# Products of the down rows of blocks 0 and 1 scheduled at high priority at their anchors

## Chip, cores and metric

The kernel runs on one core of a Trainium2 chip. The metric is the device time of one execution in microseconds (us). The kernel before takes 3732.13 us, the median of three runs (3730.72 to 3739.1).

## What is computed

One decoder layer over 1024 tokens of width 1024, all in float32. Two mixers run in parallel on the normed input (sliding-window attention with sinks, and an mLSTM in chunks), are gated, summed and projected (`w_out`), and added to the input: this is x2. Behind it stands a PEER expert layer. For every token and each of 8 heads, two lists of 128 scores give a top 16 of 16384 experts; then, cut to what matters here:

```
idx  = take_along_axis(cand_i, best_pos)                 # 8 heads x 16 experts of a token
gate = softmax(best_s)
act  = gelu(einsum('td,thkd->thk', xb, expert_down[idx]))   # the down rows
out  = einsum('thk,thkd->td', gate * act, expert_up[idx])   # the up rows
```

## The kernel before, in words

The 1024 tokens are 8 blocks of 128. The program has two parts.

**The front** goes over four groups of two blocks (0 and 1, 2 and 3, 4 and 5, 6 and 7). For each group `front` computes projections, attention, mLSTM, gates, x2 and the scores of the experts. Weights come in 512 KB parts on SP's DMA queue (L224, three buffers). In 200 of the 328 parts the weight is split: ACT rounds it (`whi`, L232), DVE takes the rest (`wlo`, L233), and TensorE (PE) runs three matmuls (L249 to L251); the others (outputs of the mixers, `w_out`, the query) go straight to L247. The last step of a group on DVE is the sum with x, L632. Behind each group's front the previous group's `topk` is written (DVE, L671 to L723) and, for blocks 2 to 5, `spread` (DVE L756 and L759 build one-hot rows, PE L764 multiplies them, the result goes to `gate_d`). `later` gives both a priority number that is 5000 larger, that is, they come after the front where both are ready.

**The dense part** (`dense`, L840 on) computes all 16384 experts for blocks 2 to 5 by matmuls (L856 and others), and beside it the gathered rows of blocks 1, 6 and 7.

Blocks 0 and 1 get their down products in the front. `down` (L777) does it: POOL gathers one expert row for each of the 128 tokens by an indirect DMA of 512 KB (L772), DVE multiplies it with xb and sums it into a column of `act` (L785), 128 times for a block. The gathers have three buffers (`gp`), so a gather waits for the product that stands three places before it. Block 1 waits for block 0 at `act` and `xb`, which have one buffer. From block 0's products come its coefficients (Gelu on ACT, L789; L790 on DVE), and `scatter` adds them into the table `coef_d` by 128 indirect DMAs from POOL (L801), in 8 heads of 16, each head after the one before has landed. Block 0 then takes part in the dense matmuls.

What sets the order: the program is written down as a trace and a list scheduler orders each engine's queue, taking among the ready instructions the one with the smallest priority number, which grows with the place in the program. The products of blocks 0 and 1 are written behind all four groups. Each carries an ordering edge (no wait on the chip) to an anchor, a matmul of the front:

```
for s in range(P):
    t = fetch(p, "down", r["idx"], s)
    ins = V.tensor_tensor_reduce(out=t, in0=t, in1=xb, ..., accum_out=act[:, s:s + 1])
    after(ins, next(pace, None))
```

The front has 664 such anchors, 166 in a group. Block 0's products are paced from 0.34 to 0.64 of them (`PACE0`, `PACE1`), block 1's from 0.64 to 0.96 (`PACE2`), the scatters from 0.66 to 0.97 (`SPREAD0`, `SPREAD1`). An anchor says only that a product does not come earlier. On the chip every engine works its queue strictly in order.

Of the kernel before, what the change touches and what calls it, by code (L numbers as in the profile page):

```python
# [23 lines left out]
P = 128  # L24
# [14 lines left out]
HALF = 0  # L39
EARLY = (1,)  # L40
# [8 lines left out]
PACE0, PACE1, PACE2 = 0.34, 0.64, 0.96  # L49
# [48 lines left out]
def build(nc, tc, a, out, dbg=None):  # L98
# [8 lines left out]
    gp = pool("gather", 3)  # L107
# [53 lines left out]
    def after(ins, name):  # L161
        if name is not None:
            tc.add_manual_dep(ins.ins, name, NOSYNC, reason="pace")
# [606 lines left out]
    def fetch(p, table, idx, s):  # L770
        t = p.tile([P, D], F32, name="g")
        G.indirect_dma_start(out=t, out_offset=None, in_=a[table],  # L772
                             in_offset=bass.IndirectOffsetOnAxis(ap=idx[:, s:s + 1], axis=0))
        return t

    def down(r, b, pace, p):
        act = bp.tile([P, P], F32, name="act", bufs=1)  # L777
        xb = bp.tile([P, D], F32, name="xb", bufs=1)
        SY.dma_start(xb, xb_d[b])
        gain = p.tile([P, D], F32, name="g")  # L780
        SY.dma_start(gain, a["gain2"].to_broadcast([P, D]))
        V.tensor_tensor(xb, xb, gain, ALU.mult)
        for s in range(P):
            t = fetch(p, "down", r["idx"], s)
            ins = V.tensor_tensor_reduce(out=t, in0=t, in1=xb, scale=1.0, scalar=0.0, op0=ALU.mult,  # L785
                                         op1=ALU.add, accum_out=act[:, s:s + 1])
            after(ins, next(pace, None))
        coef = bp.tile([P, P], F32, name="coef")
        A.activation(coef, act, AF.Gelu)  # L789
        V.tensor_tensor(coef, coef, r["gate"].rearrange("p h k -> p (h k)"), ALU.mult)  # L790
        r["coef"] = coef

    def scatter(cell, vals, pace):

        views = bass_types.dram_disjoint_views(flat[:, None], 16)
        done = []
        for h in range(8):
            new = []
            for s in range(16):
                c = 16 * h + s  # L800
                ins = G.indirect_dma_start(out=views[s], out_offset=bass.IndirectOffsetOnAxis(ap=cell[:, c:c + 1], axis=0),  # L801
                                           in_=vals[:, c:c + 1], in_offset=None, compute_op=ALU.add)
                if s == 0:
                    for d in done:
                        tc.add_manual_dep(ins.ins, d, SYNC, reason="heads")
                else:
                    after(ins, new[0])
                after(ins, next(pace, None))
                new.append(ins.ins.name)
            done = new  # L810
# [112 lines left out]
    res = {}  # L923
# [18 lines left out]
    def paced(lo, hi, n):  # L942
        return iter([names[int((lo + i * (hi - lo) / n) * len(names))] for i in range(n)])

    down(res[HALF], HALF, paced(PACE0, PACE1, P), gp)
    scatter(res[HALF]["cell"], res[HALF]["coef"], paced(SPREAD0, SPREAD1, P))
    for b in EARLY:
        down(res[b], b, paced(PACE1, PACE2, P), gp)
    inner.close()
    gd = dense()  # L950
    names = anchors["dense"]
# [19 lines left out]
```

## Time and profile before

| | |
|---|---|
| Median of three runs | 3732.13 us |
| The profiled execution | 3726.21 us, span 3724.4 us |
| Busy: PE, DVE, ACT, POOL | 87%, 74%, 36%, 37% of the span |
| Mean granted TensorE clock | 0.925 |

The profile is one execution. Busy time is by engine; idle time stands before an instruction and is put down to what ended it. `PE pj L250 <- DVE wlo L233` reads: PE waited at line 250 for what DVE writes at line 233. Times "in a stretch" are from the span's start. The stretches used below end with the last L632 of a group: group 1 is 327 to 752 us, group 2 is 752 to 1229, group 3 is 1229 to 1833; the first dense matmul starts at 1992.

### The profile page before, as it was taken

To read this page: it belongs to the slowest core of one execution; us is meant where nothing else is said; L and a number is where in the kernel's file an instruction comes from. 1 tells how busy PE (TensorE), PEld (TensorE's weight loads), DVE (VectorE), ACT (ScalarE), POOL (GpSimd) and SP (SyncE) were. 2 spreads that over 40 slices of the span, in tenths; PEclk is the share of its full clock that TensorE was granted. 3 is DMA by queue.
4 is the path that set the end of the run, shared out by engine and by line. 5 is a ranking of instruction groups with operands and counts; after the bars stand their busy time and mean duration, and the time that the engine had idled before them with its cause. 6 is when DMAs were issued, how large, how long until landed. Compare 5 with 4: busy or idle time off the path is not lost.

```text
span 3724.4 us, 49376 instructions
## 1 busy us (share of the span) xinstructions
PE 3247.9 (87%) x17248; PEld 2737.1 (73%) x17248; DVE 2762.6 (74%) x6356; ACT 1322.2 (36%) x2667; POOL 1396.2 (37%) x1028
## 2 busy tenths in 40 slices
PE   7998998779989648867567999989889999999999
PEld 7887887668778547756455777777777788777887
DVE  5331877659788347667976988878878888888886
ACT  6642664138454317321543322212212222222222
POOL 0000002310012576768000056555555555555552
PEclk9999989889899769878888999999999999999999
DMA  6444446873379867778656399989989999998995
GB/s 193 155 146 151 149 141 209 302 268 124 121 222 293 243 188 214 245 239 246 156 113 230 127 316 324 319 321 343 324 300 319 321 329 321 323 328 312 330 317 192
DMA packets 413049, 914.00 MB, mean 245 GB/s; under 512 B 179584, under 2 KB 200832, under 8 KB 408704
## 3 DMA queue, kind: packets, MB, share of 16 engines
q0 software_dynamic: 147456, 469.89, 37.4%
q1 hardware_dynamic: 265344, 440.96, 35.7%
q8 instruction: 136, 2.23, 0.2%
q14 instruction: 113, 0.93, 0.1%
HBM read 847.75 MB, written 62.98 MB: 245 GB/s over the span
## 4 chain that ended last, share of the span: by engine, by line
issue 20%; POOL 14%; DMA 12%; DVE 9%; PE 8%; ACT 1%; POOLq 0%; SPq 0%; ACTq 0%; DVEq 0%
POOL g L772 13%; DMA g<-up,idx 5%; DMA g<-down,idx 4%; PE ph L856 2%; PE at L764 1%; POOL coef_d L801 1%; DMA rawu<-up 1%; PE pj L247 1%; DVE g L785 1%; DVE ld L846 1%; PE po L886 1%; PE po L890 1%; PE po L889 1%; DVE lu L846 1%; DVE ef L711 0%
## 5 line engine op out<-in xcount | busy, mean ns | idle before, releaser
L772 POOL DMA_INDIRECT g<-down,idx x512 | 639.3, 1249 | 1469.8 <-DVE act L785 567.4
L785 DVE CUSTOM_DVE_ANT_0 g<-g,xb 128x1024 f32<-128x1024 f32 x512 | 618.7, 1222 | 347.0 <-DMA g<-down,idx 339.2
L772 POOL DMA_INDIRECT g<-up,idx x384 | 530.8, 1382 | 756.3 <-DVE y L894 371.2
L818 DVE SCALAR_TENSOR_TENSOR acc<-g,coef,acc 128x1024 f32<-128x1024 f32 x384 | 492.4, 1282 | 78.1 <-DMA g<-up,idx 68.7
L856 PE MATMUL ph<-xbh,hd 128*128 128x512 f32 x1024 | 414.0, 404 | 66.1 <-ACT hd L845 36.6
L856 PE MATMUL ph<-xbh,ld 128*128 128x512 f32 x1024 | 415.6, 406 | 33.7 <-DVE ld L846 33.6
L845 ACT CAST hu<-rawu 128x1024 fp32r<-128x1024 f32 x128 | 131.3, 1047 | 846.0 <-PE po L890 582.5
L856 PE MATMUL ph<-xbl,hd 128*128 128x512 f32 x1024 | 411.0, 401 | 0.0
L233 DVE TENSOR_TENSOR wlo<-w,whi 128x1024 fp32r<-128x1024 f32 x200 | 243.6, 1220 | 145.2 <-ACT whi L232 144.0
L232 ACT CAST whi<-w 128x1024 fp32r<-128x1024 f32 x200 | 209.2, 1047 | 392.9 <-DMA w<-wmain 246.6
L250 PE MATMUL pj<-wlo,hT 128*128 128x256 f32 x832 | 249.1, 300 | 72.7 <-DVE wlo L233 72.7
L856 PEld LDWEIGHTS ph<-xbh,hd 128*128 128x128 f32 x1024 | 200.7, 196 | 115.0 <-ACT hd L845 38.4
L856 PEld LDWEIGHTS ph<-xbh,ld 128*128 128x128 f32 x1024 | 199.8, 195 | 91.2 <-DVE ld L846 49.5
L249 PE MATMUL pj<-whi,hT 128*128 128x256 f32 x832 | 248.6, 301 | 17.5 <-ACT whi L232 17.5
L251 PE MATMUL pj<-hT,wlo 128*128 128x256 f32 x768 | 228.4, 300 | 23.9 <-DVE wlo L233 23.9
L251 PE MATMUL pj<-whi,hTlow 128*128 128x256 f32 x832 | 247.2, 298 | 0.0
L801 POOL DMA_INDIRECT coef_d<-coef,cell x128 | 225.9, 1765 | 50.6 <-issue 36.6
L249 PE MATMUL pj<-hT,whi 128*128 128x256 f32 x768 | 232.7, 304 | 8.4 <-ACT whi L232 4.3
L856 PEld LDWEIGHTS ph<-xbl,hd 128*128 128x128 f32 x1024 | 200.1, 195 | 42.4
L250 PE MATMUL pj<-hTlow,whi 128*128 128x256 f32 x768 | 228.5, 298 | 0.0
L250 PEld LDWEIGHTS pj<-wlo,hT 128*128 128x128 f32 x832 | 169.9, 204 | 76.9 <-DVE wlo L233 74.9
L846 DVE TENSOR_TENSOR lu<-rawu,hu 128x1024 fp32r<-128x1024 f32 x128 | 156.1, 1219 | 93.6 <-ACT hu L845 91.3
(290 smaller groups left out, 7666.9 us busy)
## 6 DMA issues: line engine op xcount, KB each, us to landing
w<-wmain SPq DMA_DIRECT2D x328, 512.0 KB
rawd<-downT SPq DMA_DIRECT2D x128, 512.0 KB
rawu<-up SPq DMA_DIRECT2D x128, 512.0 KB
gate_d<-stage SPq DMA_DIRECT2D x32, 1024.0 KB
g<-gate_d SPq DMA_DIRECT2D x32, 1024.0 KB
x<-x SPq DMA_DIRECT2D x16, 512.0 KB
coef_d<-none SPq DMA_DIRECT2D x128, 64.0 KB
sc_d<-sc SPq DMA_DIRECT2D x16, 512.0 KB
```

The costliest lines, as they stand in the source:

```text
L232: A.copy(hi, t)
L233: V.tensor_tensor(lo, t, hi.bitcast(F32), ALU.subtract)
L249: T.matmul(ps, lh(c), rh(c), start=first, stop=False)
L250: T.matmul(ps, lh(c), rl(c), start=False, stop=False)
L251: ins = T.matmul(ps, ll(c), rh(c), start=False, stop=last)
L772: G.indirect_dma_start(out=t, out_offset=None, in_=a[table], in_offset=bass.IndirectOffsetOnAxis(ap=idx[:, s:s + 1], axis=0))
L785: ins = V.tensor_tensor_reduce(out=t, in0=t, in1=xb, scale=1.0, scalar=0.0, op0=ALU.mult, op1=ALU.add, accum_out=act[:, s:s + 1])
L801: ins = G.indirect_dma_start(out=views[s], out_offset=bass.IndirectOffsetOnAxis(ap=cell[:, c:c + 1], axis=0), in_=vals[:, c:c + 1], in_off ...
L818: ins = V.scalar_tensor_tensor(acc, t, g, acc, ALU.mult, ALU.add)
L845: A.copy(hi, raw)
L846: V.tensor_tensor(lo, raw, hi.bitcast(F32), ALU.subtract)
L856: ins = T.matmul(ps, w[:, c, :], x[:, c, :], start=first, stop=last)
```

## The change

`down` of blocks 0 and 1 is traced in `tc.high_priority()`, so that its instructions go ahead of all others that are ready. The call of block 1 is moved in front of `scatter`. Anchors, paces, buffers and arithmetic stay.

```
-    down(res[HALF], HALF, paced(PACE0, PACE1, P), gp)
+    with tc.high_priority():
+        down(res[HALF], HALF, paced(PACE0, PACE1, P), gp)
+        for b in EARLY:
+            down(res[b], b, paced(PACE1, PACE2, P), gp)
     scatter(res[HALF]["cell"], res[HALF]["coef"], paced(SPREAD0, SPREAD1, P))
-    for b in EARLY:
-        down(res[b], b, paced(PACE1, PACE2, P), gp)
```

No instruction is added or taken away on DVE, PE, POOL or SP; the last 2069 rows of DVE's queue, 6977 of PE's and 655 of POOL's, which hold the dense part, stand as before. Counted from the two orders, DVE's queue up to the last L632 of each group holds:

| DVE rows | group 1 | group 2 | group 3 | then, up to the first dense step |
|---|---|---|---|---|
| products L785, before | 57 | 61 | 138 | 0 |
| products L785, now | 58 | 105 | 93 | 0 |
| topk + spread, before | 353 + 0 | 344 + 428 | 187 + 244 | 207 + 224 |
| topk + spread, now | 353 + 0 | 302 + 224 | 381 + 448 | 55 + 224 |

The first product stands at DVE's row 784 (before: 948), the last of block 0 at 1758 (before: 2435).

**POOL's queue from the first gather on.** The gathers are `g<-down,idx`, the scatters `coef_d<-coef,cell`. Before:

```order
L772 DMA g<-down,idx 128x1024 x128
L801 DMA coef_d<-coef,cell 2097152x1 x16
L772 DMA g<-down,idx 128x1024 x2
L801 DMA coef_d<-coef,cell 2097152x1 x16
L772 DMA g<-down,idx 128x1024 x2
L801 DMA coef_d<-coef,cell 2097152x1 x6
L772 DMA g<-down,idx 128x1024 x3
```

and now:

```order
L772 DMA g<-down,idx 128x1024 x139
L801 DMA coef_d<-coef,cell 2097152x1
L772 DMA g<-down,idx 128x1024
L801 DMA coef_d<-coef,cell 2097152x1
L772 DMA g<-down,idx 128x1024
L801 DMA coef_d<-coef,cell 2097152x1
```

Two heads of 16 scatters stood between block 1's first gathers. Now 11 gathers of block 1 stand before the first scatter, and from there scatters and gathers take turns. 25 scatters stand before the last gather of group 2 (before: none).

**DVE's queue around block 0's coefficients** (L790; `act` is the column of sums, L782 makes block 1's xb ready). Before:

```order
L785 ISA g,act<-g,xb 128x1024
L785 ISA act 128x1
L790 TENSOR_TENSOR coef<-coef,gate 128x128
L782 TENSOR_TENSOR xb<-xb,g 128x1024
L785 ISA g,act<-g,xb 128x1024
L785 ISA act 128x1
L785 ISA g,act<-g,xb 128x1024
L785 ISA act 128x1
```

and now:

```order
L673 MAX_INDEX ti<-tv,sc 128x8
L790 TENSOR_TENSOR coef<-coef,gate 128x128
L673 MAX_INDEX ti<-tv,sc 128x8 x3
L675 MATCH_REPLACE sc<-tv,sc 128x128 x3
L756 TENSOR_SCALAR oi<-iota,cols 128x128
L782 TENSOR_TENSOR xb<-xb,g 128x1024
L756 TENSOR_SCALAR oi<-iota,cols 128x128
L785 ISA g,act<-g,xb 128x1024
```

The products stood in a row, behind the work of topk and spread of group 2. Now they stand among it, and that work comes later by as much.

**DVE's queue at the last L632 of group 3.** Before:

```order
L756 TENSOR_SCALAR oi<-iota,cols 128x128
L759 TENSOR_SCALAR oj<-iota,cols 128x128
L632 TENSOR_TENSOR x<-pj,x 128x512 x2
L677 MAX tv<-sc 128x8
L679 MAX_INDEX ti<-tv,sc 128x8 x4
L688 TENSOR_TENSOR cand<-tv 128x2x16
```

and now:

```order
L717 TENSOR_REDUCE gsum<-dgate 128x8
L632 TENSOR_TENSOR x<-pj,x 128x512
L703 TENSOR_SCALAR ef<-bpf 128x32
L707 TENSOR_TENSOR eq<-bpf,iota 128x544
L704 TENSOR_TENSOR bpf<-bpf,ef 128x32
L718 RECIPROCAL gsum<-gsum 128x8
```

Before, a whole block of spread stood ahead of these sums and most of the topk of block 5 behind them. Now that topk is nearly done there, and 448 rows of spread, two blocks' worth, stand in group 3 ahead of them.

## Rows read from the trace of the kernel before

**Rows 1.** The page's share of engines, and of the chain that ended last.

```profile
PE 3247.9 (87%) x17248; PEld 2737.1 (73%) x17248; DVE 2762.6 (74%) x6356; ACT 1322.2 (36%) x2667; POOL 1396.2 (37%) x1028
issue 20%; POOL 14%; DMA 12%; DVE 9%; PE 8%; ACT 1%; POOLq 0%; SPq 0%; ACTq 0%; DVEq 0%
```

**Rows 2.** Busy time by stretch: group 1, group 2, group 3, the passage to the dense part, the dense part.

```profile
core 0: us, PE busy (x) PEld busy (x) DVE busy (x) ACT busy (x) POOL busy (x), PEclk, DMA share, GB/s
327.00:752.00 425.00, 371.38 (x2362) 324.73 (x2362) 285.22 (x942) 185.49 (x431) 61.78 (x60) 0.90 0.57 197
752.00:1229.00 477.00, 433.15 (x2829) 378.91 (x2830) 386.88 (x1373) 258.39 (x618) 65.57 (x61) 0.93 0.67 210
1229.00:1833.00 604.00, 435.03 (x2606) 376.87 (x2605) 385.83 (x1093) 214.05 (x493) 392.71 (x263) 0.83 0.75 217
1833.00:2000.00 167.00, 86.41 (x482) 70.31 (x483) 122.97 (x557) 66.58 (x168) 0.00 (x0) 0.74 0.58 166
2000.00:3724.40 1724.40, 1618.46 (x6899) 1314.49 (x6897) 1445.96 (x2026) 428.43 (x575) 875.92 (x640) 0.97 0.85 301
```

**Rows 3.** What DVE waited for longest, in groups 1, 2 and 3 in this order, a line for each: us in total, times, longest.

```profile
DVE g L785 <- DMA g<-down,idx: 54.5, 33, 5.0
...
DVE g L785 <- DMA g<-down,idx: 37.1, 19, 7.1
...
DVE g L785 <- DMA g<-down,idx: 189.6, 75, 31.1
```

**Rows 4.** DVE in order of time at the start of group 3 and at its end: start, duration, line, and in brackets the idle time before.

```profile
1257.15 0.29 DVE L790 TENSOR_TENSOR coef<-coef,gate 128x128 f32<-128x128 f32 x1 [0.38 <-ACT coef L789]
1263.09 1.23 DVE L782 TENSOR_TENSOR xb<-xb,g 128x1024 f32<-128x1024 f32 x1 [5.64 <-DMA g<-gain]
...
1295.41 1.23 DVE L785 CUSTOM_DVE_ANT_0 g<-g,xb 128x1024 f32<-128x1024 f32 x1 [31.10 <-DMA g<-down,idx]
...
1326.80 1.22 DVE L785 CUSTOM_DVE_ANT_0 g<-g,xb 128x1024 f32<-128x1024 f32 x1 [28.97 <-DMA g<-down,idx]
...
1831.25 1.29 DVE L632 TENSOR_TENSOR x<-pj,x 128x512 f32<-128x512 f32 x2
```

**Rows 5.** POOL in order of time at the start of group 3, in the same form.

```profile
1257.73 1.60 POOL L801 DMA_INDIRECT coef_d<-coef,cell  x1 [7.43 <-DVE coef L790]
...
1286.43 1.55 POOL L801 DMA_INDIRECT coef_d<-coef,cell  x1 [0.30 <-DMA coef_d<-coef,cell]
1288.28 1.00 POOL L772 DMA_INDIRECT g<-down,idx  x1 [0.30 <-issue]
1289.59 0.97 POOL L772 DMA_INDIRECT g<-down,idx  x1 [0.31 <-issue]
1292.33 1.60 POOL L801 DMA_INDIRECT coef_d<-coef,cell  x1 [1.78 <-DMA coef_d<-coef,cell]
...
1320.60 1.55 POOL L801 DMA_INDIRECT coef_d<-coef,cell  x1 [0.30 <-issue]
1322.45 1.00 POOL L772 DMA_INDIRECT g<-down,idx  x1 [0.30 <-issue]
```

**Rows 6.** POOL's two groups of instructions between 1257 and 1771 us: busy, mean ns of one, idle before.

```profile
L801 POOL DMA_INDIRECT coef_d<-coef,cell x128 | 225.9, 1765 | 50.6 <-issue 36.6 <-DVE coef L790 7.4 <-DMA coef_d<-coef,cell 6.2
L772 POOL DMA_INDIRECT g<-down,idx x128 | 159.2, 1244 | 86.5 <-DVE act L785 29.0 <-issue 20.1 <-DVE es L461 11.2
```

**Rows 7.** What PE waited for in group 3 (the first two lines) and in the passage behind it (the last two).

```profile
PE pj L250 <- DVE wlo L233: 71.5, 8, 45.0
PE pj L251 <- DVE wlo L233: 16.4, 4, 5.3
...
PE tp L745 <- DVE ef L711: 45.4, 2, 44.5
PE ph L856 <- ACT hd L845: 19.8, 1, 19.8
```

**Rows 8.** DVE's products alone (L785) by stretch: groups 1, 2 and 3. Two records make a product.

```profile
327.00:752.00 425.00, 70.12 (x114) 0.90 0.57 197
752.00:1229.00 477.00, 74.32 (x122) 0.93 0.67 210
1229.00:1833.00 604.00, 169.25 (x276) 0.83 0.75 217
```

**Rows 9.** Busy time of the 67 us before the last L632, in which DVE's queue holds the 244 rows of spread and almost nothing else.

```profile
1764.00:1831.00 67.00, 53.83 (x330) 44.43 (x329) 65.94 (x292) 40.59 (x102) 7.26 (x5) 1.00 0.65 142
```

**Rows 10.** What PE waited for longest in group 2.

```profile
PE tp L287 <- ACT scr L309: 12.4, 1, 12.4
```

**Rows 11.** The products of L785 in group 1 (583 to 750 us) and between 1340 and 1765 us: how many, duration, first and last start; and DVE's idle time before them, us and times.

```profile
L785 DVE CUSTOM_DVE_ANT_0 g<-g,xb x57: 1172/1225/1270, 583.4 to 749.1; 128x1024 f32<-128x1024 f32 x57
  DMA g<-down,idx: 54.5, 33
...
L785 DVE CUSTOM_DVE_ANT_0 g<-g,xb x124: 1194/1224/1298, 1342.1 to 1762.4; 128x1024 f32<-128x1024 f32 x124
  DMA g<-down,idx: 116.8, 67
```

**Rows 12.** Two pieces of the chain that ended last: a scatter and a gather from issue to landing.

```profile
1386.09 2.40 DMA coef_d<-coef,cell
...
1460.49 7.10 DMA g<-down,idx
```

## The prediction

> **What bounds the kernel now.** The page's first part says PE 87% and DVE 74% of the span, and the chain that ended last belongs to POOL, DMA and "issue" more than to PE or DVE [rows 1]. So the mean hides stages; I read it by stages [rows 2]. The dense part (2000 to 3724 us) keeps PE busy 1618 of 1724 us, and no queue order in it changes. The front is another matter: groups 1, 2 and 3 take 425, 477 and 604 us. Group 3 holds the same front for PE as group 2, and PE and DVE are busy as long in both (435 and 433 us; 386 and 387), yet it lasts 127 us longer. POOL is the column that differs: 393 against 66 us.
>
> The waits tell why. DVE waits for gathers 54.5, 37.1 and 189.6 us in groups 1, 2 and 3 [rows 3]. In order of time the reader sees how: at 1257.73 POOL begins block 0's scatters, 16 in a row, issues two gathers at 1288.28 and 1289.59, then 16 more scatters, and the next gather only at 1322.45 [rows 5]. DVE, in order, stands before the products of those gathers for 31.1 and 29.0 us [rows 4], and behind the products in its queue stand the `wlo` that PE needs: PE waits for `wlo` 71.5 and 16.4 us, once 45.0 [rows 7]. Afterwards POOL is the slowest: 225.9 + 159.2 us busy of the 514 from 1257 to 1771, and 36.6 + 20.1 more in issue gaps of 0.3 us [rows 6]. That is **442 us of POOL work in 514**, and the 138 products of group 3 go at its pace. The granted clock is 0.83 in group 3 and 0.93 in group 2 [rows 2]: PE idles before the clock falls.
>
> **The change, part by part.** Nothing is added. What moves are products, and topk and spread in the opposite direction; counts are those of the table of DVE's rows.
>
> *Prices.* A product is 169.25 / 138 = 1.23 us of DVE [rows 8]. A row of spread: DVE is busy 65.9 us in a stretch that holds 244 of them, 0.27 us [rows 9]; I take this for topk as well (207 + 224 rows of both stand in 123 us of the passage, 0.28 or less [rows 2]).
>
> *DVE work.* Group 2: 387 + 44 products x 1.23 - 246 rows x 0.27 = 387 + 54 - 66 = 375 us. Group 3: 386 - 45 x 1.23 + 398 x 0.27 = 386 - 55 + 107 = 438 us. The passage: -152 x 0.27 = -41 us.
>
> *Idle time of DVE that is not for gathers.* Group 2 has 477 - 387 - 37 = 53 us, waiting for PE, ACT and weights. Group 3 has 604 - 386 - 190 = 28, since gathers were later than anything else there. I take 53 for both, as POOL no longer bounds group 3.
>
> *Waits for gathers, w a product.* This is the unknown. Measured: 54.5 / 57 = 0.96 in group 1, where products came every (749 - 583) / 57 = 2.9 us; 116.8 / 124 = 0.94 between 1342 and 1762, one every 3.4 us, with scatters between [rows 11]; 37.1 / 61 = 0.61 in group 2 [rows 3, 8]; all of group 3 gives 189.6 / 138 = 1.37 with the two large stalls. A gather is issued when the product three places earlier is done, so the wait falls as products stand further apart. Spread over the stretches that I forecast they come every 480 / 105 = 4.6 and 538 / 93 = 5.8 us, wider than in any of these rows. The bounds are 0 (three periods of 4.6 us cover the 7.1 us that a gather took [rows 12]) and 1.37; I take 0.5, a little under the nearest row, 0.61, because the anchors still bunch where the weights are not split (4 matmuls to an anchor there, elsewhere 12). Group 2: 105 x 0.5 = 52; group 3: 47.
>
> *Group 2 becomes 375 + 53 + 52 = 480 us (+3), group 3 becomes 438 + 53 + 47 = 538 us (-66).* PE's 435 and POOL's 93 gathers and some 100 scatters (93 x 1.54 + 100 x 2.07 = 350 us with the gaps, [rows 6]) fit into 538.
>
> *The passage.* Now PE waits 44.5 us for DVE's `ef`, the last topk of block 5 [rows 7], because 207 rows of topk stand behind the sums at 1831 [rows 4]. 55 remain. What is late next is ACT's `scr` for PE's transposes, 12.4 us at the same place of group 2 [rows 10]. So -32 us, with bounds 0 (the spread of block 5 still follows) and -45. The 19.8 us that the first dense matmul waits for ACT [rows 7] stay.
>
> *Edits at nothing.* Group 1 keeps 58 products and all its topk; they start earlier and should wait a little less, at most 54.5 / 2 = 27 us, which I leave for the range. Block 1's load of xb and gain and the coefficients cost DVE 0.4 + 5.6 us and POOL 7.4 before [rows 4, 5]; they come once in either order, only earlier. Products ahead of `wlo` on DVE delay it by 1.23 us each, covered by three weight buffers; without that cover it is 1.23 us x 105 in group 2, the products' DVE time that is already in the sum.
>
> *Sum:* +3 - 66 - 32 = -95 us on the profiled execution's 3726.2 us, 3631. The median of the runs stands 5.9 us above that execution: **3637 us**. As a formula: groups 2 and 3 take 919 + 198 w against 1081, and the passage gives 32; w = 0.98 would leave the time as it is.
>
> **The rivals.**
>
> *A. Slower: gathers mixed with scatters land late.* Nearly every gather of block 1 now has a scatter just before it on POOL, and its product stands among front and spread work that it holds up. Were block 1's 128 products to wait 1.37 us each, as in all of group 3, and block 0's 70 in group 2 0.5: 919 + 175 + 35 = 1129, less 32, against 1081: +16 us, 3748. It decides from a mean w of 0.98. For it: a scatter took 2.40 us to land in the chain [rows 12]. Against it: from 1342 to 1762 gathers and scatters alternate already, and w is 0.94 there against 0.96 without a scatter [rows 11]. The Trainium skill says, in "DMA: Bandwidth & Descriptors", section "SWDGE vs HWDGE vs iDMA", that only one queue is allocated for the DMAs that GpSimd's software issues; so a gather would stand behind its scatter's data there too. By that rule I should add up to the scatter's landing to each gather, which is this rival; the rows just named do not bear it out.
>
> *B. More: the waits all but vanish.* With w = 0.2, the passage at -45 and group 1 at -27: 919 + 40 - 1081 - 45 - 27 = -194, 3538 us. For it: three periods cover a gather. Against it: PE alone is busy 433 of 477 us in group 2, so that group can lose little; -194 asks 449 of it. A higher granted clock would help PE in group 3 (0.83 now).
>
> *C. No change: the waits move.* DVE's queue up to the first dense step holds the same work in either order, so the front shortens only by the waits that DVE loses. If products in front of `wlo`, `sg` and x sums make PE wait in many small pieces what it waited in three large ones, w stays near 0.98 and the time at 3726 to 3738. Against it: the 31.1 and 29.0 us have no cause any more, as no 16 scatters stand in a row.
>
> **How the numbers follow.** Chances: forecast 0.62 (w from 0.3 to 0.85), B 0.14, C 0.10, A 0.14. Low end: w = 0.25 and the passage at -45, 919 + 50 - 1081 - 45 = -157, 3575, a little lower for group 1's part: 3565. High end: w = 0.95 without gain in the passage beyond 32 gives -6; I go to 3730 to take in most of C. A measurement can tell about 0.2% (7.5 us) from no change. Faster by more takes in the forecast, B and half of C: 0.81; within 0.06; slower 0.13.
>
> **What would show it.** Group 3 shorter by 40 to 90 us; no wait of DVE for a gather above some 12 us; PE's wait for `wlo` in group 3 below 30 us; POOL's scatters beginning in group 2; the wait for `ef` below 15 us; group 2 within 25 us of 477. I am wrong if DVE's waits for gathers in groups 2 and 3 together stay above 190 us, or if group 2 grows by what group 3 loses.

## The result, and the profile after

The changed kernel takes 3630.24 us (median of four runs, 3628.07 to 3639.16) against 3731.43 for the kernel before: ratio **0.973, 95% interval 0.971 to 0.975**. Timed again beside other kernels (run e9 below) it gave 0.976 (0.974 to 0.978). The profiled execution has a span of 3626.3 us, 98 less than before.

The page's two rows that answer to [rows 1]: shares of the engines, and of the chain that ended last.

```profile
PE 3258.4 (90%) x17248; PEld 2746.8 (76%) x17248; DVE 2764.2 (76%) x6356; ACT 1320.9 (36%) x2666; POOL 1404.4 (39%) x1028
PE 30%; issue 22%; DMA 16%; DVE 14%; POOL 13%; ACT 4%; SPq 0%; POOLq 0%; ACTq 0%; DVEq 0%
```

The work is the same to some 10 us an engine; the chain now has PE and DVE ahead of POOL. The stretches again end with the last L632 of a group (329, 736, 1215, 1773 us), and the first dense matmul starts at 1891.9 (before: 1992.2). Busy time by stretch, as in [rows 2]: groups 1, 2, 3, the passage with the first dense matmuls, the dense part.

```profile
329.00:736.00 407.00, 371.16 (x2362) 325.80 (x2362) 286.10 (x944) 185.61 (x429) 69.80 (x61) 0.91 0.60 206
736.00:1215.00 479.00, 408.66 (x2573) 354.40 (x2573) 374.32 (x1180) 215.60 (x505) 175.38 (x131) 0.91 0.76 244
1215.00:1773.00 558.00, 465.71 (x2860) 405.62 (x2860) 437.84 (x1495) 260.36 (x623) 288.48 (x193) 0.87 0.74 209
1773.00:1900.00 127.00, 83.03 (x483) 68.23 (x484) 82.65 (x346) 61.73 (x150) 0.00 (x0) 0.83 0.69 199
1900.00:3626.30 1726.30, 1624.97 (x6898) 1319.73 (x6896) 1447.40 (x2023) 428.32 (x575) 870.57 (x640) 0.97 0.85 300
```

Columns are PE, PEld, DVE, ACT and POOL busy, then clock, DMA share and GB/s. Group 3 is 46 us shorter than in [rows 2], the passage 40 (119 to the first dense matmul, before 159), group 1 18; group 2 is 2 longer. DVE is busy 374 and 438 us in groups 2 and 3, POOL 175 and 288 where it was 66 and 393. DVE's waits for gathers in groups 1, 2 and 3, as in [rows 3], with the wait for `whi` that exceeds them in group 1 (50.1 us, before 48.9) and the next two of group 3:

```profile
DVE wlo L233 <- ACT whi L232: 50.1, 12, 29.9
DVE g L785 <- DMA g<-down,idx: 28.6, 18, 3.1
...
DVE g L785 <- DMA g<-down,idx: 54.7, 32, 4.4
...
DVE g L785 <- DMA g<-down,idx: 55.8, 27, 6.1
DVE wlo L233 <- ACT whi L232: 30.6, 9, 10.8
DVE oj L759 <- PE at L764: 13.8, 17, 5.1
```

The waits for gathers are 139 us in all (before 281), the longest 6.1 us. What PE waited for in group 3 (two lines) and in the passage (two lines), as in [rows 7]:

```profile
PE tp L745 <- DVE ef L711: 18.4, 2, 17.5
...
PE pj L250 <- DVE wlo L233: 8.6, 4, 4.0
...
PE ph L856 <- ACT hd L845: 19.7, 1, 19.7
...
PE tp L745 <- DVE ef L711: 4.2, 2, 2.3
```

The wait for `wlo` has gone from 71.5 to 8.6; the one for `ef` has moved into group 3 and is 17.5 us long where it was 44.5. POOL in order of time where the scatters begin, as in [rows 5]:

```profile
1110.38 1.00 POOL L772 DMA_INDIRECT g<-down,idx  x1 [2.92 <-DVE oi L756]
1111.69 1.94 POOL L801 DMA_INDIRECT coef_d<-coef,cell  x1 [0.30 <-issue]
1115.08 1.92 POOL L772 DMA_INDIRECT g<-down,idx  x1 [1.45 <-DVE oj L759]
1117.30 1.58 POOL L801 DMA_INDIRECT coef_d<-coef,cell  x1 [0.30 <-issue]
1119.19 0.98 POOL L772 DMA_INDIRECT g<-down,idx  x1 [0.31 <-DVE oi L756]
```

The first scatter goes out at 1111.7, 146 us earlier than before, inside group 2, and they take turns with the gathers.

### The profile page after: what moved, and what is told of

Same layout as the page of the kernel before. It is cut to its first block, busy times and chain, and to the rows that moved or that the text cites. A ratio compares the mean times of both kernels' runs of the same rounds, so it can differ in the third digit from the quotient of the medians.

```text
span 3626.3 us, 49307 instructions
## 1 busy us (share of the span) xinstructions
PE 3258.4 (90%) x17248; PEld 2746.8 (76%) x17248; DVE 2764.2 (76%) x6356; ACT 1320.9 (36%) x2666; POOL 1404.4 (39%) x1028
## 4 chain that ended last, share of the span: by engine, by line
PE 30%; issue 22%; DMA 16%; DVE 14%; POOL 13%; ACT 4%; SPq 0%; POOLq 0%; ACTq 0%; DVEq 0%
POOL g L772 12%; PE pj L247 6%; DMA g<-up,idx 5%; DMA g<-down,idx 5%; PE ph L856 3%; DVE g L785 3%; PE pj L249 2%; DMA w<-wmain 2%; PE pj L251 2%; PE at L764 2%; PE pj L250 2%; DMA rawu<-up 2%; POOL coef_d L801 1%; PE tp L287 1%; PE po L886 1%
## 5 line engine op out<-in xcount | busy, mean ns | idle before, releaser
L785 DVE CUSTOM_DVE_ANT_0 g<-g,xb 128x1024 f32<-128x1024 f32 x512 | 618.8, 1220 | 195.7 <-DMA g<-down,idx 194.4
L856 PEld LDWEIGHTS ph<-xbh,ld 128*128 128x128 f32 x1024 | 202.1, 197 | 80.8 <-DVE ld L846 38.2
L764 PE MATMUL at<-oj,oi 128*128 128x128 f32 x1024 | 174.7, 305 | 36.7 <-ACT oj L762 26.3
```

The costliest lines, as they stand in the source:

```text
L764: T.matmul(ps[:, 2 * u + n, :], oi[:, n], oj[:, n], start=True, stop=True)
L856: ins = T.matmul(ps, w[:, c, :], x[:, c, :], start=first, stop=last)
```

## The experiments

Two theories stood at the start. **T:** group 3 goes at the pace of POOL's queue, and the change pays because less of POOL's work falls into group 3. **Rivals:** the two long runs of scatters are the whole of it (R1), or only the earlier topk of block 5, in the passage (R2). All ratios are against the kernel before, timed beside each run. The changed kernel's own two ratios, 0.973 and 0.976, lie some 10 us apart, so a difference of that size tells nothing between kernels that were not timed side by side. Lengths of stages and waits are those of one profiled execution each, the passage counted to the first dense matmul. POOL's work is its busy time plus the 0.3 us gap of each DMA.

| kernel | ratio | groups 1, 2, 3, passage (us) | waits for gathers in 1, 2, 3 | POOL's work in group 3 |
|---|---|---|---|---|
| before | 1 | 424, 477, 605, 159 | 54.5, 37.1, 189.6 | 472 |
| e1 order only | 1.000 | 422, 476, 622, 142 | 54.5, 38.2, 197.5 | 467 |
| e2 block 1 high | 0.988 | 422, 476, 612, 114 | 54.6, 34.4, 144.4 | 463 |
| e3 block 0 high | 0.973 | 406, 499, 532, 126 | 28.7, 40.0, 106.3 | 388 |
| e7 e3, late scatter | 0.982 | 409, 499, 564, 125 | 30.4, 42.9, 140.7 | 439 |
| e4 before, no scatter | 0.973 | 427, 475, 520, 140 | 60.6, 35.2, 82.7 | 207 |
| changed | 0.973 | 407, 479, 558, 119 | 28.6, 54.7, 55.8 | 346 |
| e5 changed, no scatter | 0.966 | 408, 471, 537, 118 | 29.1, 45.3, 17.4 | 129 |
| e6 changed, 2 buffers | 0.997 | 443, 511, 575, 119 | 67.4, 86.9, 88.7 | 346 |
| e8 block 0 to 0.58 | 0.970 | 437, 473, 538, 100 | 48.9, 45.7, 25.9 | 292 |
| e11 e3 with e8's paces | 0.968 | 436, 493, 491, 120 | 50.3, 52.3, 80.2 | 344 |
| e12 e8, ends earlier | 0.980 | 440, 495, 584, 66 | 52.5, 57.2, 49.0 | 266 |

### One part of the change alone: e1, e2, e3

**e1.** Block 1's down is only written ahead of the scatter.

```
     down(res[HALF], HALF, paced(PACE0, PACE1, P), gp)
-    scatter(...)
     for b in EARLY:
         down(res[b], b, paced(PACE1, PACE2, P), gp)
+    scatter(...)
```

> No high priority; block 1's down is only written ahead of the scatter. DVE's rows of groups 1 and 2 stay as before, group 3 keeps its 138 products and all 128 scatters; POOL's first run of scatters is 11 (before: 16), then 3 (before: 16); 143 rows of topk are left for the passage (before: 207). Theory T (group 3 goes at the pace of POOL, and the waits for gathers are what the change takes away): the two stalls of 31 and 29 us shrink to about 20 and 5, the pace of POOL stays, and 64 rows of topk move from the passage (-17 us) into waits of group 3. About -40 us (-25 to -60), group 3 about 570. Rival R1 (the two long runs of scatters are the whole of it): most of the 100 us, -70 or more. Rival R2 (the gain is the earlier topk of block 5 in the passage): -17 us and group 3 unchanged.

Measured: ratio 1.000 (0.998 to 1.002). The first two stalls did shrink as T said, to 20.7 and 5.0 us, but a new one of 30.1 us stands further on: DVE in order of time in e1.

```profile
1284.15 1.23 DVE L785 CUSTOM_DVE_ANT_0 g<-g,xb 128x1024 f32<-128x1024 f32 x1 [20.67 <-DMA g<-down,idx]
1291.67 1.23 DVE L785 CUSTOM_DVE_ANT_0 g<-g,xb 128x1024 f32<-128x1024 f32 x1 [4.96 <-DMA g<-down,idx]
...
1451.17 1.23 DVE L785 CUSTOM_DVE_ANT_0 g<-g,xb 128x1024 f32<-128x1024 f32 x1 [30.10 <-DMA g<-down,idx]
```

Before the last of them POOL issues 22 scatters in a row, with no gather between: the first, the last and the gather behind them.

```profile
1398.31 1.69 POOL L801 DMA_INDIRECT coef_d<-coef,cell  x1 [0.30 <-issue]
...
1445.08 1.55 POOL L801 DMA_INDIRECT coef_d<-coef,cell  x1 [0.30 <-issue]
1446.94 1.00 POOL L772 DMA_INDIRECT g<-down,idx  x1 [0.30 <-issue]
```

The waits of group 3 sum to 197.5 us (before 189.6). DVE has 15 us more work in group 3, and the group is 17 us longer, which is what the passage gained. So the -40 was wrong. POOL still has some 467 us to do in group 3, and a wait that was taken away in one place came back in another. R1 is not tested by this run: the long runs of scatters moved, they did not go.

**e2.** High priority for block 1 alone.

```
     down(res[HALF], HALF, paced(PACE0, PACE1, P), gp)
+    with tc.high_priority():
+        for b in EARLY:
+            down(res[b], b, paced(PACE1, PACE2, P), gp)
     scatter(...)
-    for b in EARLY:
-        down(res[b], b, paced(PACE1, PACE2, P), gp)
```

> High priority for block 1's products alone. Groups 1 and 2 as before; group 3 keeps 138 products and all 128 scatters, but no more than 3 scatters stand in a row near its start; 52 rows of topk are left for the passage (before 207, with the change 55). T: POOL's 442 us of work still fall into group 3, so the wait stays near 0.9 us a product and group 3 takes 572 to 600 us; the passage gives its 40; in all -45 to -75 us. R1 (only the long runs of scatters matter): both parts come in full, -95 us or more, as with the whole change. R2 (only the passage): -40 us, group 3 stays at 604.

Measured: 0.988 (0.984 to 0.992), some 46 us. Group 3 and the passage of e2, by stretch, and then DVE's longest wait in group 3:

```profile
1231.00:1843.00 612.00, 437.19 (x2610) 380.28 (x2609) 430.26 (x1313) 220.57 (x513) 384.47 (x263) 0.81 0.75 220
1843.00:1957.00 114.00, 75.73 (x467) 64.29 (x467) 71.73 (x308) 60.74 (x148) 0.00 (x0) 0.90 0.69 192
```

```profile
DVE g L785 <- DMA g<-down,idx: 144.4, 64, 14.2
```

The time is at the low edge of T's range, the stages are not as T said: group 3 is not shorter, though no wait is above 14.2 us, and all of the gain is the passage's 45, which is R2's figure. R1 asked for 95 us or more and falls: the waits above 8 us are down from 71 us to 24, and 121 us of shorter ones are left. DVE does 43 us more in group 3 and waits 45 us less. Whether the shorter stalls made room for this work, or any wait would have taken it in, the run does not tell; in e1 work that moved into group 3 was not free.

**e3.** High priority for block 0 alone.

```
-    down(res[HALF], HALF, paced(PACE0, PACE1, P), gp)
+    with tc.high_priority():
+        down(res[HALF], HALF, paced(PACE0, PACE1, P), gp)
     scatter(...)
```

> High priority for block 0's products alone; block 1 stands behind the scatter at low priority. Group 2 has 78 products (before 61, with the change 105) and all of its 772 rows of topk and spread, group 3 has 120 products, and 14 scatters stand in a row; 86 rows of topk are left for the passage. T: group 2 is 387 + 21 + 53 + 47 = 508 us (+31), group 3 386 - 22 + 33 + 40 + 120 x 0.94 + 25 for the one long run = 575 (-29), the passage -33: about -30 us (-60 to 0). R1: one long run of scatters is left, so half of the gain, -45 to -55. R2: -33 from the passage and nothing else.

Measured: 0.973 (0.970 to 0.977), the whole gain; every expectation was too small. Groups 2 and 3 of e3:

```profile
739.00:1238.00 499.00, 448.42 (x2826) 384.38 (x2826) 408.21 (x1406) 260.15 (x619) 142.75 (x107) 0.92 0.73 220
1238.00:1770.00 532.00, 420.73 (x2608) 366.29 (x2607) 396.50 (x1232) 214.94 (x506) 322.12 (x218) 0.87 0.79 233
```

The forecast of DVE's work held (408 and 397 us); what fell away is the waits, 106 us for 120 products where 138 was expected (0.94 each and 25 for one long run). The first scatter goes out at 1050 us, and 28 of them stand in group 2.

### Is it when POOL scatters, or where the products stand? e7, e4, e5

**e7.** As e3 (high priority for block 0, not shown again), with the scatters paced later. The products stand on DVE as in e3.

```
-SPREAD0, SPREAD1 = 0.66, 0.97
+SPREAD0, SPREAD1 = 0.76, 0.97
```

> As the kernel with high priority for block 0 alone (run e3, ratio 0.9732), but the scatters are paced from 0.76 of the anchors where they were from 0.66. The products stand on DVE as in e3 (58, 78, 120; 83 rows of topk left for the passage); no scatter falls into group 2, all 128 into group 3, behind 39 of its 120 gathers. T (group 3 goes at POOL's pace, and it matters how much of POOL's work falls into it): 120 x 1.54 + 128 x 2.07 = 450 us of POOL work in group 3 against some 397 in e3; at the share that POOL reached in group 3 before, 442 of 514, that takes 523 us, and with the start and the end of the group about 565: 25 to 45 us slower than e3, ratio 0.980 to 0.986. Rival P (it is the earlier products that count, not when POOL scatters): as e3, 0.973.

Measured: 0.982 (0.980 to 0.984), some 34 us slower than e3 by the two ratios, inside T's range and clear of the rival's. Groups 2 and 3 of e7, and DVE's longest wait in group 3:

```profile
742.00:1241.00 499.00, 452.71 (x2824) 388.49 (x2824) 406.19 (x1403) 259.32 (x618) 97.38 (x78) 0.91 0.69 219
1241.00:1805.00 564.00, 427.63 (x2611) 372.22 (x2609) 399.99 (x1234) 220.62 (x510) 365.05 (x245) 0.84 0.77 219
```

```profile
DVE g L785 <- DMA g<-down,idx: 140.7, 69, 5.7
```

Group 2 is the same 499 us and DVE's busy time the same to 4 us; 28 scatters of POOL moved from group 2 into group 3, and group 3 grew from 532 to 564 with 34 us more waits, none of them above 5.7 us. So it matters when POOL scatters, and it takes no long stall to cost time. In before, e1, e2 and e7 POOL's work is 75 to 78% of group 3's length. That this is the pace of its queue is read from the share and not shown: in e7 POOL itself waits 84.5 us there for products that free a buffer.

e7 also says what the scatters' time does not explain. Its first scatter goes out at 1349 us, later than in the kernel before, and it is still 65 us faster than that kernel. This larger part of the gain comes with block 0's products done earlier: 120 of them in group 3 where 138 were, group 3 41 us shorter, the passage 34, group 1 15, group 2 22 longer.

**e4 and e5.** The scatters left out, in the kernel before and in the changed one; block 0's expert part is missing from the output.

```
-    scatter(res[HALF]["cell"], res[HALF]["coef"], paced(SPREAD0, SPREAD1, P))
```

> The kernel before without the 128 scatters, so block 0's expert part is left out of its output; all products, gathers and dense matmuls are there. POOL has 159 + 20 us of work in group 3 instead of 442. T: group 3 is 386 + 66 x 0.27 + 53 + 138 x 0.55 = 533 us (-71), the passage (141 rows of topk) -18: about -90 us (-60 to -110). R2 (passage only): -18 us. A rival to T on POOL, that gathers are late for the rate of the DMA engines and not for POOL's queue: the waits of group 3 stay above 120 us and the time falls by less than 60.

> The changed kernel without the 128 scatters; block 0's expert part is left out of its output, everything else stands as in the changed kernel (DVE's rows by group are the same). T (before, POOL's queue bounds group 3; after the change it does not): the waits for gathers in groups 2 and 3 fall from 55 + 56 us by some 15 to 35, and the time by as much: -115 to -135 us against the kernel before, 10 to 35 below the changed one. Rival (the scatters cost what they cost wherever they stand, as traffic or as work on POOL): they are again worth about 100 us, that is -200 against the kernel before.

Measured: 0.973 (0.970 to 0.977) and 0.966 (0.965 to 0.968), both within T's ranges. Group 3 in e4 and in e5:

```profile
1230.00:1750.00 520.00, 425.63 (x2609) 368.39 (x2608) 403.19 (x1187) 217.72 (x504) 166.44 (x135) 0.87 0.79 258
```

```profile
1211.00:1748.00 537.00, 457.46 (x2860) 398.22 (x2860) 435.73 (x1497) 259.75 (x624) 102.16 (x91) 0.89 0.69 217
```

The same 128 scatters cost about 100 us before the change and about 26 after it (3630.2 against 3603.9 in medians; 28.5 in spans). So the change takes away some three quarters of what they cost, and the rival that they cost the same anywhere falls. By e7 some 34 of these 76 us are a matter of when they are done; no run separates the rest. The rival to POOL, the rate of the DMA engines, falls with e4's waits of 82.7 us in group 3, where it asked for more than 120.

Without any scatter the same change still gives some 20 us (3624.0 to 3603.9): group 1 and the passage are 19 and 22 us shorter, group 3 is 17 longer.

### Does a wait of DVE cost what it lasts? e6

```
-    gp = pool("gather", 3)
+    gp = pool("gather", 2)
```

> The changed kernel with two gather buffers for the front's down rows where it has three; DVE's rows by group move by 15 at most. A gather can then start only when the product two places before it is done. T, by the prediction's sum (groups 2 and 3 take 919 us plus the waits): the waits for gathers rise by 0.5 to 1 us a product, 130 to 250 us over the three groups, and the time grows by as much as the waits do. Rival (waits of DVE are slack that other work fills, and only POOL's pace counts): the waits rise as much, and the time by less than half of it.

Measured: 0.997 (0.995 to 0.999). DVE's longest wait in groups 1, 2 and 3 of e6:

```profile
DVE g L785 <- DMA g<-down,idx: 67.4, 35, 5.3
...
DVE g L785 <- DMA g<-down,idx: 86.9, 52, 4.2
...
DVE g L785 <- DMA g<-down,idx: 88.7, 48, 4.8
```

The waits rise by 104 us, less than the 130 to 250 expected (0.41 us a product, not 0.5 to 1), and the span by 86.9: 0.84 for one. In groups 1 and 2 it is nearly all of it (39 and 32 us of waits, 36 and 32 of length), in group 3 half (33 and 17). So in groups 1 and 2 a wait costs about what it lasts, as the prediction's sum takes it, and in group 3 half of it is covered.

### Can more be had? e8 to e12

**e8**, and again as **e10** beside the changed kernel (**e9**): block 0 is done earlier.

```
-PACE0, PACE1, PACE2 = 0.34, 0.64, 0.96
-SPREAD0, SPREAD1 = 0.66, 0.97
+PACE0, PACE1, PACE2 = 0.34, 0.58, 0.96
+SPREAD0, SPREAD1 = 0.60, 0.97
```

> The changed kernel with block 0's products paced from 0.34 to 0.58 (0.64), block 1's from 0.58, the scatters from 0.60. Products by group 73, 105, 78 (58, 105, 93); 131 + 50 rows of spread and topk are left for the passage (224 + 55). T: group 1 has 15 more products of 1.23 us and closer ones, +20 us; group 3 has 15 fewer, but 73 more rows of topk and spread, +1 for DVE and 10 less in waits; the passage is 98 x 0.27 = 26 us of DVE shorter, of which PE's wait for DVE there (4 us) can give little. About the same as the changed kernel, -15 to +15. Rival (the sooner POOL is free, the better): 20 us or more below the changed kernel.

> The changed kernel itself, timed on the same chip as the next three so that they can be compared with it: ratio 0.973, as before.

> The kernel of run e8 (block 0 paced to 0.58) beside the changed kernel. Its stages in e8 were 30 us more in group 1, 6 less in group 2, 20 less in group 3 and 19 less in the passage. T: those differences are the products, POOL's work and the topk and spread that moved, and repeat: 10 to 20 us below the changed kernel, ratio 0.968 to 0.971. Rival: e8 and the changed kernel differ by the scatter of the runs only, ratio 0.972 to 0.974.

Measured: e8 0.970 (0.968 to 0.972); on one chip, e9 0.976 (0.974 to 0.978) and e10 0.968 (0.966 to 0.970). That is 27 us in medians below the changed kernel (3638.2 and 3611.2), more than T's 10 to 20; what came is the rival of e8, the sooner POOL is free, the better. In e8 group 1 pays 30 us for more and closer products, groups 2 and 3 and the passage give 45 back.

**e11.** The same paces, high priority for block 0 alone.

> High priority for block 0 alone, with the paces of e8 (products 73, 73, 110 by group; 42 scatters in group 2; 56 + 224 rows of topk and spread left). T: group 1 as in e8 (437 us), group 2 402 us of DVE + 53 + 73 x 0.55 = 495, group 3 with 110 x 1.54 + 86 x 2.07 = 347 us of POOL work no longer bound by it: 520, the passage 124: about 10 to 20 us above the changed kernel, ratio 0.975 to 0.979. Rival (the earlier POOL is free, the better): below e3 and e8, 0.968 or less.

Measured: 0.968 (0.966 to 0.969), 3608.9 us: better than the changed kernel, the best median here of a kernel that computes the whole layer, and not to be told from e10. It is the rival's forecast that came, not T's. T's stages sum to 36 us more than the profile has, 29 of them in group 3. Group 3 of e11:

```profile
1258.00:1749.00 491.00, 415.44 (x2609) 361.32 (x2609) 391.19 (x1250) 219.92 (x513) 286.36 (x192) 0.89 0.81 241
```

Against e3 POOL has 44 us less to do in group 3 and group 3 is 41 shorter. This fits a group 3 that POOL's queue still held back in e3; ten products left it as well.

**e12.** Block 1 is done earlier as well.

```
-PACE0, PACE1, PACE2 = 0.34, 0.58, 0.96
-SPREAD0, SPREAD1 = 0.60, 0.97
+PACE0, PACE1, PACE2 = 0.34, 0.58, 0.90
+SPREAD0, SPREAD1 = 0.60, 0.92
```

> As e8, and block 1's products end at 0.90 of the anchors (0.96), the scatters at 0.92: products 73, 114, 69; 19 + 50 rows of spread and topk are left for the passage (131 + 50). T: group 2 has 9 more products, +11 of DVE and 5 of waits; group 3 has 9 fewer and 140 more rows of topk and spread, +27; the passage loses 112 rows, -30 of DVE, but no wait of PE for them is left there to be won (4 us in the changed kernel): 0 to 20 us above e8. Rival (what leaves the passage is won in full): 10 to 30 us below e8.

Measured: 0.980 (0.979 to 0.982), 42 us above e10, more than T's 0 to 20, and the rival that what leaves the passage is won in full falls. The passage falls to 66 us and group 3 grows to 584. Group 3 and the passage of e12:

```profile
1264.00:1848.00 584.00, 490.84 (x3095) 425.13 (x3095) 461.20 (x1663) 295.95 (x713) 222.22 (x147) 0.89 0.70 190
1848.00:1914.00 66.00, 40.53 (x232) 35.19 (x232) 22.18 (x98) 26.05 (x59) 0.00 (x0) 0.86 0.66 225
```

POOL is far from a bound here (266 us of 584) and waits for gathers are 49. PE and DVE are both at their busiest, 491 and 461 us, with the topk and spread that moved in: group 3 seems long by its own work here, which no run shows by itself.

## Why the prediction was right, by its steps

Forecast 3637 us, measured 3630; forecast -95 us on the profiled execution, measured -98 in span.

**DVE's work: right.** 375 and 438 us were forecast for groups 2 and 3, the profile has 374.3 and 437.8. Prices of 1.23 us a product and 0.27 a row, times a count from the two orders, were enough. The stretch of [rows 9] was misread: by line it holds 223 rows of spread and some of topk, not 244 of spread alone. The price of 0.27 still gave the sums to within a us.

**Waits for gathers: right in size.** w = 0.5 was taken; it is 54.7 / 105 = 0.52 in group 2 and 55.8 / 93 = 0.60 in group 3. The reason given, wider spacing, would have the smaller w in group 3. In e5, without scatters, it does: 45.3 / 105 = 0.43 and 17.4 / 93 = 0.19. So 0.41 of group 3's 0.60 goes with the scatters, which the 0.5 did not count; that it came near there is luck.

**Group 2 (+3): +2. Group 3 (-66): -46.** The term that was too large is group 3, by 9 us through the waits (55.8, not 47) and by 11 through idle time that is not for gathers: 558 - 438 - 56 = 64 us where 53 was taken. The 53 were group 2's of before, where waits for `whi` are 25.0 us and L759's waits for PE's spread matmuls (L764) 6.3; in group 3 they are now 30.6 and 13.8, which covers the 11. PE's own load there is 466 us (before 435), since the spread matmuls moved into group 3 with DVE's rows. The prediction said that PE's 435 fit and did not count these.

**The passage (-32): -40.** The wait for `ef` there is 4.2 us (before 45.4), less than the 12.4 that I allowed for `scr`. But a wait of 17.5 for `ef` now stands in group 3, so "below 15 us" was wrong as a sign of it; the other five signs came.

**Group 1 (0): -18.** This was left for the range. Its waits fell from 54.5 to 28.6. e3 and e7, which start the products at the same place, have it too (28.7, 30.4); e1 and e2 do not. With the passage's 8 us it covers the 20 that group 3 lacks, so the total is nearer than its terms: that is luck.

**The cause: half right.** The prediction saw that POOL's work held group 3 back: without the scatters the kernel before gains 102 us and the changed one 26. It also said that the 31.1 and 29.0 us vanish "as no 16 scatters stand in a row". They did, but e2 and e7 show that the runs are not the point: with no wait above 14.2 and 5.7 us, waits of 144 and 141 us are left in group 3 as long as all 128 scatters fall into it. What pays is that block 0 is done earlier. Of e3's 100 us some 34 come from scatters that begin sooner (e7), and the rest with the earlier products. Block 1's high priority alone gives 46 us (e2), but adds nothing that the runs can tell once block 0 has it (e3 and the changed kernel 0.973; e11 and e10 0.968).

**Rivals.** A (mixed gathers land late) did not come: in group 3 of the changed kernel the 70 gathers that POOL issues right behind a scatter land 5.4 us after their start (median), the 21 behind another gather 6.6. The Trainium skill, in "DMA: Bandwidth & Descriptors", section "SWDGE vs HWDGE vs iDMA", has one queue for the DMAs that GpSimd's software issues. These landings show no delay behind a scatter in it. The scatters' part of the waits is thus not a late landing; it fits gathers that are issued later. B did not come: w stayed at 0.5 to 0.6. C did not for this change; e1, the new order without the priority, took the time that C forecast.

Open: what bounds group 3 once POOL does not. PE and DVE are both at 78 to 84% there in the changed kernel and in e12, and no run here separates them.

## What to carry to other kernels

When an in-order engine waits for many transfers, ask how much of that stage the queue that issues them is at work. Where it is most of it, a stall that is removed can come back further on (e1), and many short waits cost as much as a few long ones (e7). Move the issuing queue's work into a stage where that queue is idle, which is often a matter of when its first input is ready. And a move has two ends: count what it pushes into the stage that follows, on every engine.

## What the runs showed that was not expected

Two buffers where there were three cost only 0.41 us of wait a product, with the products 4 to 6 us apart (0.67 in group 1, 0.31 and 0.35 in groups 2 and 3). The scatters take 3.0, 5.5 and 9.2 us (shortest, median, longest) from issue to landing in the changed kernel, longer than the 2.40 of the one piece in [rows 12], and gathers behind them land no later for it. The mean granted clock of group 3 went with PE's idle time there: 0.83 before, with 169 us idle, 0.81 in e2 with 175, and 0.89 in e11 with 76.
